# A hybrid decoder block: 64 bytes more in the tile hst, ahead of the weight slots

## The chip, the cores and the metric

The kernel runs on one core of one Trainium2 chip. Its time is the device time of one execution in microseconds (us), taken as the median of several runs. The profile is of one further execution. Five engines work side by side, each in its own order: TensorE (PE, whose weight loads are listed apart as PEld), VectorE (DVE), ScalarE (ACT), GpSimd (POOL) and SyncE (SP, which issues most DMAs). A matmul has a stationary operand, the weights, which a load of its own brings into the array, and a moving operand, whose rows stream past.

## What is computed

One layer of a decoder block for 2048 positions of 1024 channels. A projection `x @ W_in + b_in` with 72 x 128 output columns feeds two branches: dilated windowed attention with three head groups, and a gated linear recurrence (RG-LRU). Both are gated, merged, projected and normalised.

```
proj = x @ w_in[l] + b_in[l]
q, k, v, g_attn, u_lru, g_lru, gate_logits = jnp.split(proj, SPLIT_POINTS, axis=-1)
...
y_a = attn @ w_attn_proj[l]
...
u = causal_depthwise_conv(u_lru, conv_w[l], conv_b[l])
h = rg_lru(u, lru_wr[l], lru_br[l], lru_wi[l], lru_bi[l], lru_lambda[l]).astype(dt)
y_b = (h * jax.nn.silu(g_lru)) @ w_lru_proj[l]
...
merged = gates[:, :, 0] * y_a + gates[:, :, 1] * y_b
out = merged @ w_out[l] + b_out[l]
x = layer_norm(DEEPNORM_ALPHA * x + out, ln_gain[l], ln_bias[l])
```

In the recurrence, each position needs the state of the one before; the kernel works in chunks of 512 positions, and keeps each chunk's last column for the next.

## The kernel before, in words

**Three stages.** The first, up to about 1443 us, is the projection (the matmuls of line 647), with the recurrence woven in. The second, up to about 1837 us, is the attention and the product yb (line 1241). The last is ya (lines 1513 to 1515), the output product z (lines 1546 to 1548) and the normalisation.

**A pass of the projection.** The positions are taken in two halves, and in each half 36 passes s run over pairs of 128 output columns: 72 passes. Most passes use a scheme with seven products in place of eight: the two column blocks and the two halves of the 1024 channels make 2 x 2 blocks of weights, the channels and two chunks of 512 positions make 2 x 2 blocks of x, and sums of blocks are multiplied. The blocks of x, B11, B21, B12, B22 and the sums T1 to T4, appear in the profile as xB and xT, the weights as hA and hS, after the block or sum that they hold. Four passes, the first two of each half, run plainly with eight products. Their order is the list PLAIN, whose last two products both use B22:

```
PLAIN = [(fi, k, c) for c in range(2) for k in range(2) for fi in range(2)]
MID, EDGE = (1, 6, 7, 5, 2, 4, 3), (1, 2, 6, 7, 4, 5, 3)
```

In the other passes the last product, number 3, uses B22. The six others use blocks of x elsewhere.

**A product** (`product`) is 12 matmuls into one PSUM bank: for each of four groups of 128 channels the three terms high weights by high x, high weights by low x, low weights by high x. Such a triple reads as h, h, l in the profile. Every matmul brings its own weight load, which is 128 columns of 4 bytes (512 bytes a partition), while the moving operand has 512 columns (2048 bytes a partition). After six matmuls of a product the gates of the recurrence (lines 505 and 509: 6 matmuls each time, 32 times in all) may be put in.

**What sets the order.** The program is written out by hand for all engines: a loop of ticks, one product a tick, in which weights of later passes are loaded by SP, split into a high part by ACT (line 284) and a low part by DVE or POOL (line 240), results are taken out of PSUM, and chains of follow-up work are advanced.

**Where the operands stand.** Tiles of a pool follow each other in each partition, each beginning at a multiple of 32 bytes. Ahead of the pool sl_p stands the pool X, with six blocks of 16,384 bytes: seven of the eight blocks of x live there at one time or another, and all begin at the same place modulo 256. Then sl_p, in this order: slot 0 (2048 bytes), `ubs` (288), `hst` (64), the three tiles `ub0` to `ub2` of the recurrence (2064 each, so 2080), and the other 34 slots, the four tiles lo0 to lo3 for low weights (4096 each) and the block of B22, called XA (16,384), in the order of their first use. High weights take any free slot. The kernel takes 2048, 4096 or 16,384 bytes for each of these, so they all begin at one place modulo 256. Between the end of slot 0 and that place lie 288 + 64 + 3 x 2080 = 6592 = 25 x 256 + 192 bytes. So modulo 256:

- the six X blocks and slot 0 begin at one place;
- the other slots, the lo tiles and B22's block begin 64 bytes short of it;
- steps within them (512 bytes a weight tile, 2048 a moving row) are multiples of 256 and change nothing.

In the second and third stage sl_p is given up. The pools that follow begin where X ends, and the operands of yb, ya and z stand at the place of the X blocks, weights and moving rows alike.

`hst` holds for each of the eight channel tiles of the recurrence the last column of a chunk. It is cleared at the start (line 441), read as the initial state of the scan (line 546), and written by line 547. Only column 0 of its last dimension is used.

Of the kernel before, what the change touches and what calls it, by code (L numbers as in the profile page):

```python
# [8 lines left out]
F32 = mybir.dt.float32  # L9
# [6 lines left out]
P = 128  # L16
# [15 lines left out]
def hybrid_block_kernel(ctx: ExitStack, tc: tile.TileContext, a: dict, out: bass.AP):  # L32
# [111 lines left out]
    sl_p = stA.enter_context(tc.tile_pool(name="sl_p", bufs=1))  # L144
# [291 lines left out]

    lrn = cst.tile([P, 4, 8], F32, name="lrn")
    ubs = sl_p.tile([P, 8, 3, 3], F32, name="ubs")
    hst = sl_p.tile([P, 8, 2], F32, name="hst")
    dve.memset(ubs, 0.0)  # L440
    dve.memset(hst, 0.0)
    ub_free = [sl_p.tile([P, CH + 4], F32, name=f"ub{j}") for j in range(3)]
# [1228 lines left out]
```

## Time and profile before

| | |
|---|---|
| median of 3 runs | 2108.59 us (2106.66 to 2108.61) |
| the profiled execution's own time | 2111.93 us |
| its span | 2110.1 us |
| granted clock, mean | 0.997 |
| first stage, matmuls of line 647 | 7.2 to 1443.2 us, 6096 of them |
| DVE busy | 1695.4 us |
| DMA moved | 444.06 MB |

The span runs from the first to the last instruction of the profiled execution; that execution took 3.34 us more than the median. Times in the views are microseconds from the start of the span, unless marked ns. In the page, "xN" is a count, and an engine's busy share is of the whole span. A row of the timeline gives start, length, engine, line, operation, names (out<-in) and shape, and merges neighbours of one kind: "x2" are the two h terms of a triple. The ends of matmuls are modelled and overlap the next one's start; the starts are what is to be compared. A row of the windows gives the stretch, its length, busy time and number of instructions for each engine, then the granted clock, the share of the DMA engines' time and GB/s.

### The profile page before, as it was taken

Reading aid. Unit: us, or ns where it says so; the run is one execution under the profiler, and the core shown is the slowest. Engines: PE = TensorE matmul, PEld = TensorE weight load, DVE = VectorE, ACT = ScalarE, POOL = GpSimd, SP = SyncE. Lnnn points to the kernel's source line nnn. Section 1 sums busy time; section 2 is a strip of 40 time slices with the busy share of each in tenths; the row PEclk is TensorE's granted clock in tenths of the full one; section 3 lists DMA queues with packets and bytes.
Section 4 is the critical chain, followed back from the end, with each engine's and each line's share of the span. In section 5 each row is a group of like instructions: output and inputs, shape, how many; then the busy total and the mean of one; then the engine's idle time right before and its main releaser. Section 6 shows DMA issues by size and latency. Waiting matters only on the chain.

```text
span 2110.1 us, 35268 instructions
## 1 busy us (share of the span) xinstructions
PE 2088.1 (99%) x11877; PEld 1692.6 (80%) x11877; DVE 1695.4 (80%) x2985; ACT 1192.7 (57%) x2459; POOL 761.1 (36%) x685
## 2 busy tenths in 40 slices
PE   9999999999999999999999999999999999999998
PEld 7888888888888888888787888887878878788886
DVE  8878988999888858889788798975666776877667
ACT  6455455476457456767668877875666664321100
POOL 2554654545554201121120111114447678521120
PEclk9999999999999999999999999999999999999999
DMA  7877877788877766666657476669878886774431
GB/s 241 238 236 207 249 234 209 227 265 256 250 225 224 261 190 186 196 208 198 191 176 230 155 221 201 210 191 289 208 213 233 214 245 194 228 243 155 150 100 70
DMA packets 334180, 444.06 MB, mean 210 GB/s; under 512 B 164800, under 2 KB 174816, under 8 KB 330928
## 3 DMA queue, kind: packets, MB, share of 16 engines
q1 hardware_dynamic: 317360, 409.36, 62.2%
q0 software_dynamic: 11744, 23.54, 6.0%
q10 hardware_dynamic: 4896, 8.92, 1.1%
q8 instruction: 94, 1.54, 0.3%
q14 instruction: 86, 0.70, 0.1%
HBM read 290.20 MB, written 151.52 MB: 209 GB/s over the span
## 4 chain that ended last, share of the span: by engine, by line
PE 88%; DMA 3%; POOL 2%; SPq 2%; issue 2%; DVE 1%; ACT 1%; ACTq 0%; POOLq 0%; DVEq 0%
PE q L647 65%; PE yb L1241 4%; PE z L1547 3%; PE z L1546 3%; PE z L1548 3%; PE o L1071 2%; PE pt L1038 2%; PE s L1007 1%; PE g L505 1%; PE ya L1514 1%; PE ya L1515 1%; PE ya L1513 1%; POOL hx L1217 1%; DMA mg_scr<-y 1%; SPq L828 1%
## 5 line engine op out<-in xcount | busy, mean ns | idle before, releaser
L647 PE MATMUL q<-xT,hS 128*128 128x512 f32 x1632 | 507.0, 392 | 0.0
L647 PE MATMUL q<-xT,l 128*128 128x512 f32 x1088 | 426.9, 392 | 0.0
L647 PE MATMUL q<-xB,hA 128*128 128x512 f32 x1344 | 418.7, 393 | 0.0
L647 PE MATMUL q<-xB,l 128*128 128x512 f32 x944 | 370.5, 392 | 0.1
L647 PEld LDWEIGHTS q<-xT,hS 128*128 128x128 f32 x1632 | 305.7, 188 | 68.9 <-issue 4.0
L647 PEld LDWEIGHTS q<-xB,hA 128*128 128x128 f32 x1344 | 252.1, 188 | 57.1 <-issue 2.9
L647 PEld LDWEIGHTS q<-xT,l 128*128 128x128 f32 x1088 | 204.3, 188 | 46.9
L240 POOL TENSOR_TENSOR sw<-sw,sin 128x512 f32<-128x512 f32 x96 | 153.6, 1606 | 183.4 <-ACT sw L338 148.8
L647 PEld LDWEIGHTS q<-xB,l 128*128 128x128 f32 x944 | 177.2, 188 | 42.0 <-DVE l L240 0.5
L1023 ACT ACTIVATE pb<-pb 128x192 f32<-128x192 f32 (+1 forms) x384 | 160.7, 421 | 27.0 <-DVE pb L1021 27.0
L240 POOL TENSOR_TENSOR y<-y,h 128x512 f32<-128x512 f32 x27 | 35.6, 1318 | 383.9 <-DVE h L546 338.8
L647 PE MATMUL q<-xT,hA 128*128 128x512 f32 x544 | 169.5, 393 | 0.0
L647 PE MATMUL q<-xB,hS 128*128 128x512 f32 x544 | 169.3, 392 | 0.0
L284 ACT ACTIVATE hA<-wA 128x512 fp32r<-128x512 f32 x220 | 137.6, 636 | 38.2 <-PE q L647 17.4
L1241 PE MATMUL yb<-hx,wl 128*128 128x512 f32 x576 | 150.2, 401 | 1.9 <-POOL hx L1217 1.8
L240 POOL TENSOR_TENSOR l<-wA,hA 128x512 fp32r<-128x512 f32 x68 | 105.5, 1551 | 113.1 <-ACT hA L284 94.0
L284 ACT ACTIVATE hS<-S 128x512 fp32r<-128x512 f32 x170 | 108.2, 637 | 67.2 <-DVE S L240 52.3
L1241 PEld LDWEIGHTS yb<-hx,wl 128*128 128x128 f32 x576 | 104.9, 188 | 31.0 <-issue 6.1
L647 PEld LDWEIGHTS q<-xT,hA 128*128 128x128 f32 x544 | 101.7, 188 | 24.0 <-issue 2.6
L647 PEld LDWEIGHTS q<-xB,hS 128*128 128x128 f32 x544 | 102.1, 188 | 22.7
L1517 POOL TENSOR_TENSOR me<-gA,me 128x512 f32<-128x512 f32 x30 | 47.8, 1610 | 157.7 <-DVE gA L1516 135.4
L1546 PE MATMUL z<-wo,ms 128*128 128x512 f32 x256 | 99.6, 389 | 0.0
(215 smaller groups left out, 4307.5 us busy)
## 6 DMA issues: line engine op xcount, KB each, us to landing
wA<-in_w_in_dram SPq DMA_DIRECT2D x220, 256.0 KB
wl_scr<-l SPq DMA_DIRECT2D x102, 512.0 KB
l<-wl_scr SPq DMA_DIRECT2D x102, 512.0 KB
wS<-in_w_in_dram SPq DMA_DIRECT2D x102, 256.0 KB
wS<-in_w_in_dram POOLq DMA_DIRECT2D x68, 256.0 KB, 6.1
wlr<-in_w_f_dram SPq DMA_DIRECT2D x64, 256.0 KB
mg_scr<-y SPq DMA_DIRECT2D x59, 256.0 KB
v_scr<-vs SPq DMA_DIRECT2D x48, 256.0 KB
```

The lines of the kernel that those rows point to most:

```text
L240: eng.tensor_tensor(out=out, in0=in0, in1=in1, op=op)
L284: act.activation(heads(h), heads(r, False), AF.Copy)
L505: pe.matmul(g, gw[hs, l], x[hs], start=(n == 0), stop=(n == 2))
L647: pe.matmul(bank, w[:, ks], x[:, kk, xx], start=(first and i == 0), stop=(last and i == 11))
L1023: act.activation(pp, pp, AF.Exp, scale=-1.0, bias=mm, accum_out=ll)
L1038: pe.transpose(pt[e][:, b, 2 * h + x, :], pdata(p, h, c, c + P)[hs], ident[hs, hs])
L1071: pe.matmul(o[hs, 2 * i + b, :], (V[:, kb // 8, kb // 2 % 4, kb % 2] if g == 2 else V[:, kb % 2, kb // 4, kb // 2 % 2])[:, 64 * h:64 * h + ...
L1241: pe.matmul(YB["t"], w[:, a, k], hx(8 * c + k)[:, b], start=(hf == 0 and m == 0), stop=(hf == 1 and m == 11))
L1517: (dve if i in (6, 7) else pool).tensor_tensor(out=ME[c][:, f], in0=ga, in1=ME[c][:, f], op=ALU.add)
L1546: pe.matmul(z, mh[:, k], w[:, 0, hs], start=(k == 0), stop=False)
L1547: pe.matmul(z, mh[:, k], w[:, 1, hs], start=False, stop=False)
L1548: pe.matmul(z, ml[:, k], w[:, 0, hs], start=False, stop=(k == 7))
```

## The change

One number: the last dimension of `hst` is 4 in place of 2. Only column 0 is used as before. The tile takes 128 bytes a partition and not 64, and all that follows it in sl_p begins 64 bytes later; the X blocks, slot 0 and `ubs` stay. No instruction is added, removed or moved on any engine; the memset of line 441 covers 32 elements a partition and not 16.

```diff
     ubs = sl_p.tile([P, 8, 3, 3], F32, name="ubs")
-    hst = sl_p.tile([P, 8, 2], F32, name="hst")
+    hst = sl_p.tile([P, 8, 4], F32, name="hst")
     dve.memset(ubs, 0.0)
     dve.memset(hst, 0.0)
```

## The prediction

> **What bounds the kernel now.** First the page: its span, the busy share of each engine, the granted clock, and the chain of work that ended last.
>
> ```profile
> span 2110.1 us, 35268 instructions
> PE 2088.1 (99%) x11877; PEld 1692.6 (80%) x11877; DVE 1695.4 (80%) x2985; ACT 1192.7 (57%) x2459; POOL 761.1 (36%) x685
> ...
> PEclk9999999999999999999999999999999999999999
> ...
> PE 88%; DMA 3%; POOL 2%; SPq 2%; issue 2%; DVE 1%; ACT 1%; ACTq 0%; POOLq 0%; DVEq 0%
> ```
>
> The clock is granted in every slice, and 88% of the chain is TensorE itself. Next the busy time by stretches (us of the stretch, then busy us and instructions of PE and of PEld for line 647 alone) and the waits of PE up to 1450 us.
>
> ```profile
> 0.00:1450.00 1450.00, 1407.20 (x6096) 1143.13 (x6096) 1.00 0.72 219
> ```
>
> ```profile
> PE first_bank L858 <- ACT warm L850: 3.2, 1, 3.2
> PE pt L1038 <- ACT pb L1023: 1.3, 2, 1.2
> PE s L1001 <- DVE y L240: 0.4, 1, 0.4
> ```
>
> All 6096 matmuls of the projection lie in the first 1450 us, and no wait of PE for another engine is listed for line 647. So the projection lasts as long as 6096 matmuls follow each other, and the question is how closely they do. The page's busy time cannot tell, since the ends of matmuls are modelled. The starts can. Here is the timeline of PE over five products of one pass (start us, us, engine, line), first row and the row that begins the next product, both of the three-matmul pattern h, h, l:
>
> ```profile
> 467.83 0.62 PE L647 MATMUL q<-xT,hS 128*128 128x512 f32 x2
> ...
> 481.56 0.63 PE L647 MATMUL q<-xB,hS 128*128 128x512 f32 x2
> ```
>
> Between them stand 20 triples in 13.73 us: **0.6865 us a triple**, 228.8 ns a matmul. Weights and moving rows differ by 64 bytes (modulo 256) in these products. The same form of matmul (128 rows, 128 columns, 512 moving columns, three terms) runs in the last stage as z:
>
> ```profile
> 2057.56 0.39 PE L1546 MATMUL z<-wo,ms 128*128 128x512 f32 x1
> ...
> 2068.44 0.39 PE L1546 MATMUL z<-wo,ms 128*128 128x512 f32 x1
> ```
>
> 16 triples in 10.88 us: **0.6800 us a triple**, 226.7 ns a matmul, without an exception:
>
> ```profile
> L647 PE MATMUL q<-xT,hS x1632: 387/392/503, 54.2 to 1439.8; 128*128 128x512 f32 x182
> ...
> L1546 PE MATMUL z<-wo,ms x256: 389/389/389, 1861.2 to 2100.4; 128*128 128x512 f32 x128
> ```
>
> (least, median and longest ns of one.) For z, weights and rows begin at the same place within 256 bytes. That could be a trait of that stage, so the deciding rows are those of a product inside the projection that has the same property already: B22, whose block lies among the weight slots. In the plain pass at 737 us the last two products use it:
>
> ```profile
> 734.93 0.62 PE L647 MATMUL q<-xB,hA 128*128 128x512 f32 x2
> ...
> 737.67 0.63 PE L647 MATMUL q<-xB,hA 128*128 128x512 f32 x2
> ...
> 740.44 0.62 PE L647 MATMUL q<-xB,hA 128*128 128x512 f32 x2
> ...
> 743.16 0.63 PE L647 MATMUL q<-xB,hA 128*128 128x512 f32 x2
> ```
>
> Four triples with B12, 64 bytes apart, take 2.74 us; the first product with B22 takes 2.77, the second 2.72, which is 0.680 a triple as in z. Same engine, same line, same stage, same kind of weights; only the block changes, and the first product after the switch pays 0.05 to settle. So the spacing goes with the place modulo 256, and it needs some triples to find its state.
>
> **The change part by part.** It removes and moves no instruction. The memset of line 441 clears 32 elements a partition for 16, once, in the first microseconds, beside the loads that line 858 waits for anyway: nothing. Every tile of the pool behind hst moves up by 64 bytes, and 288 + 128 + 3 x 2080 = 6656 = 26 x 256 now lie between slot 0 and the rest: all weight slots, the four lo tiles and B22's block come to the place of the X blocks modulo 256. All 72 passes then run as the second B22 product did. Two edits come with it that I cost at nothing. The other engines mostly work from slot to slot, and these move together. DMAs into and out of slots begin 64 bytes further on; no row shows such a shift, but PE waits for none of them (the three waits above) at a DMA share of 0.72 in the windows' row, so a few per cent more or less on a transfer stay hidden; if that cover went, PE would wait for DMA by name.
>
> A whole pass of before, from the first row of one B22 product to that of the next, is 462.29 to 481.56:
>
> ```profile
> 462.29 0.63 PE L647 MATMUL q<-xB,hS 128*128 128x512 f32 x2
> ...
> 465.06 0.63 PE L647 MATMUL q<-xB,hA 128*128 128x512 f32 x2
> ...
> 465.77 0.62 PE L647 MATMUL q<-xB,hA 128*128 128x512 f32 x2
> ```
>
> It is 19.27 us for 28 triples; at 0.680 it is 19.04. The 0.23 us are 0.05 for the B22 product that has to settle (2.77 against 2.72), 0.03 for the triple behind it (0.71) and 23 triples at 0.0065. For 72 passes (four of them of 32 triples) that is 72 x 0.23 = **16.6 us**.
>
> Against it stand the interruptions. 32 pairs of gates are put into the middle of a product, and the spacing has to settle anew behind each. Now, 64 bytes apart, that is quick:
>
> ```profile
> 584.47 0.73 PE L647 MATMUL q<-xB,hA 128*128 128x512 f32 x2
> ...
> 585.27 0.62 PE L647 MATMUL q<-xB,hA 128*128 128x512 f32 x2
> ...
> 585.96 0.39 PE L647 MATMUL q<-xT,hS 128*128 128x512 f32 x1
> ```
>
> The triple behind the gates takes 0.80, the next 0.69. In the aligned state the nearest rows are yb's groups of twelve between other matmuls:
>
> ```profile
> 1473.49 3.01 PE L1241 MATMUL yb<-hx,wl 128*128 128x512 f32 x12
> 1476.43 0.46 PE L1038 MATMUL pt<-ident,pb 64*128 64x64 f32 x8
> ```
>
> 2.94 us for four triples, 0.22 over 2.72, of which the change of form at both ends has some 0.2 (the triple above has 0.11 at one end). So an interruption costs between 0.1 less and 0.1 more than now, 32 of them between -3 and +3 us; I take 0.03 each, as the B22 rows settle within 0.05: **-1.0 us**.
>
> The third term is what no longer hides. VectorE is the nearest engine behind:
>
> ```profile
> 400.00:500.00 100.00, 100.00 (x440) 81.21 (x440) 96.93 (x113) 60.23 (x100) 54.78 (x43) 1.00 0.86 253
> ```
>
> ```profile
> 372.70 0.69 DVE L537 SCALAR_TENSOR_TENSOR tr<-tr,e 128x512 f32<-128x512 f32 x1 [0.71 <-ACT sq L533]
> ...
> 398.98 1.78 DVE L240 TENSOR_TENSOR l<-wA,hA 128x512 fp32r<-128x512 f32 x1
> ...
> 401.12 0.39 PE L647 MATMUL q<-xT,l 128*128 128x512 f32 x1
> ```
>
> It is busy for 96.93 us of these 100 (third pair), and the low weights that it ends at 400.76 are read at 401.12, 0.36 us later. Its last gap was at 372.70, 28 us before, and in 28 us PE gains 1.2% (0.23 of 19.27), 0.34: the slack just holds. A wait of some tenths there and at one or two like places is what I charge: **-0.6 us**. From nothing to 4.8 us are possible (rival 2).
>
> Sum: 16.6 - 1.0 - 0.6 = 15.0 us, on the profiled execution 2111.93 - 15.0 = 2096.9. That execution lies 3.34 above the median of the runs, 2108.59, so the median to expect is **2093.6**. What follows the projection keeps its places and only begins earlier.
>
> **The rivals.** 1. No change. The spacing would go with the block or the stage and not with the place. For it: PEld shows 188 ns for a weight load everywhere, so the load itself is not slower 64 bytes apart. Against it: 2.74, 2.77 and 2.72 in three neighbouring products. It gives 2108.6. The Trainium skill has a rule that says so too (TensorE: Matmul & The Clock Gate, Step-by-step: what each phase is for): the array has two independent read ports on SBUF, and loading the next weights takes no read bandwidth from the running matmul. By it the place could not matter and the time would stay at 2108.6; the rows at 737 us speak against it.
>
> 2. VectorE becomes the bound, and takes part of the gain back. Its price is that PE gains nothing where VectorE is above 92%: the stretches 200 to 500 and 1200 to 1300 us, 400 us at 1.2% = 4.8 us.
>
> ```profile
> 200.00:300.00 100.00, 100.00 (x439) 81.41 (x438) 94.41 (x107) 53.03 (x86) 57.50 (x43) 1.00 0.83 244
> 300.00:400.00 100.00, 100.00 (x437) 81.69 (x436) 92.77 (x106) 53.27 (x85) 50.35 (x38) 1.00 0.71 216
> ...
> 1200.00:1300.00 100.00, 100.00 (x442) 80.44 (x441) 93.01 (x127) 72.77 (x116) 15.71 (x11) 1.00 0.69 213
> ```
>
> It gives 2093.6 + 4.8 = 2098.4. Against it: even 96.93 becomes only 98% of a stretch shorter by 1.2%.
>
> 3. Slower: the matmuls fall into a worse state and stay there. There is one in the trace:
>
> ```profile
> 504.73 0.63 PE L647 MATMUL q<-xB,hA 128*128 128x512 f32 x2
> ...
> 521.53 0.63 PE L647 MATMUL q<-xB,hS 128*128 128x512 f32 x2
> ```
>
> 24 triples in 16.80 us, 0.700 each. It began in a product whose weights stood in slot 0 and lasted until the next B22 product. If the aligned kernel ran in it throughout, a pass would take 19.60, 0.33 more than now, and 72 passes 23.8 us more: 2132.4. It decides the sign from the point where 0.23 x (1 - f) = 0.33 x f, f = 41% of the passes. Against it: it stands on pairs 64 bytes apart, B22 ended it, and z, always aligned, never leaves 389 ns.
>
> **How the numbers follow.** Forecast 80%: 2093.6, from 2090.5 (all 16.6 kept, with some luck in the settling) to 2097. Rival 2, or as much lost to ScalarE or transfers: 10%, 2097 to 2101. Rival 1: 6%. Rival 3: 4%. The range 2090.5 to 2099 holds the forecast's bounds and the better half of rival 2, some 85%, less what the run-to-run spread of 2 us (2106.66 to 2108.61) takes at its edges: 8 in 10. About 0.2%, 4.2 us, is what a measurement of this kernel can tell from no change. Faster by more is the forecast and rival 2, 90%; within it is rival 1, 6%; slower is rival 3, 4%.
>
> **What would show it.** Median of line 647's matmuls 389 ns, not 392, with PEld still at 188; a pass of 28 triples in 19.04 to 19.1 us; the first score matmul some 15 us earlier than now; the stages behind it as long as before; VectorE's busy time the same, on a shorter span. Wrong would be: 0.687 a triple as before (rival 1), a third spacing, new waits of PE on VectorE or ScalarE for line 647 of over 2 us in all (rival 2), or stretches at 0.700 (rival 3).

## The result, and the profile after

| | time, us | runs |
|---|---|---|
| before | 2107.62 median (2103.54 to 2108.61) | 4 |
| changed | 2091.55 median (2090.93 to 2092.82) | 4 |
| ratio | 0.9928, 95% interval 0.9911 to 0.9945 | |

The changed kernel is 16.07 us faster; the interval reaches from 11.6 to 18.8 us. The profiled execution of the changed kernel took 2092.82 us. Its page, span, busy shares, clock and chain:

```profile
span 2091.0 us, 35268 instructions
PE 2070.6 (99%) x11877; PEld 1692.0 (81%) x11877; DVE 1703.0 (81%) x2985; ACT 1191.7 (57%) x2459; POOL 764.4 (37%) x685
...
PEclk9999999999999999999999999999999999999999
...
PE 73%; DMA 3%; DVE 2%; POOL 1%; issue 1%; SPq 1%; ACT 1%; POOLq 0%; DVEq 0%; ACTq 0%
```

The count of instructions is the same, the clock is granted in every slice as before, and PEld is busy just as long (1692.0 for 1692.6). The shares of the chain can't be set side by side: they add up to 99% before and to 82% after, since the chain after could be followed back only to a row of VectorE at 388.56 us. So the 15 points that PE has less there are no finding. The page's busy time of PE is still 99% and says nothing. The view of line 647's instructions (least, median and longest ns):

```profile
L647 PEld LDWEIGHTS q<-xT,hS x1632: 186/188/190, 53.8 to 1425.8; 128*128 128x128 f32 x182
L647 PE MATMUL q<-xT,hS x1632: 389/389/501, 54.1 to 1426.1; 128*128 128x512 f32 x182
```

The matmul's median is now z's 389 ns, the weight load keeps its 188. The starts of a whole pass, in the timeline of PE:

```profile
458.62 0.61 PE L647 MATMUL q<-xB,hS 128*128 128x512 f32 x2
...
461.33 0.61 PE L647 MATMUL q<-xB,hA 128*128 128x512 f32 x2
...
464.06 0.61 PE L647 MATMUL q<-xT,hS 128*128 128x512 f32 x2
...
474.94 0.61 PE L647 MATMUL q<-xT,hA 128*128 128x512 f32 x2
...
477.65 0.61 PE L647 MATMUL q<-xB,hS 128*128 128x512 f32 x2
```

From B22 to B22 the pass takes 19.03 us (19.27 before). The product with B22 takes 2.71 and the next one 2.73, so nothing is left to settle behind the switch of the block. The 16 triples from 464.06 to 474.94 take 10.88 us, 0.680 each, z's spacing to the digit.

The projection ends where the first score matmul (line 1001) begins. Before, then after:

```profile
1443.20 0.49 PE L1001 MATMUL s<-qk 64*128 64x128 f32 x2
```

```profile
1429.33 0.48 PE L1001 MATMUL s<-qk 64*128 64x128 f32 x2
```

So the two profiled executions differ by **13.87 us** in the projection. The second stage, from there to the first ya (start of the first and of the last one in this view), before and after:

```profile
L1513 PE MATMUL ya<-at,wa x128: 388/389/397, 1839.4 to 2046.0; 128*128 128x512 f32 x128
```

```profile
L1513 PE MATMUL ya<-at,wa x128: 388/389/397, 1820.2 to 2026.9; 128*128 128x512 f32 x128
```

It lasted 396.2 us before and 390.9 after. The runs below don't show that the change speeds this stage up; these 5.3 us are one execution against one. The ya loop takes 206.6 and 206.7.

Two waits for VectorE are listed that were not listed before. The waits of PE up to 1429 us (us in total, times, longest), then rows of the timeline of PE and VectorE at both:

```profile
PE first_bank L858 <- ACT warm L850: 3.2, 1, 3.2
PE q L647 <- DVE l L240: 1.3, 2, 0.8
```

```profile
369.60 0.69 DVE L537 SCALAR_TENSOR_TENSOR tr<-tr,e 128x512 f32<-128x512 f32 x1 [0.71 <-ACT sq L533]
...
395.84 1.77 DVE L240 TENSOR_TENSOR l<-wA,hA 128x512 fp32r<-128x512 f32 x1
...
397.66 0.50 PE L647 MATMUL q<-xT,l 128*128 128x512 f32 x1 [0.75 <-DVE l L240]
...
720.43 0.50 PE L647 MATMUL q<-xB,l 128*128 128x512 f32 x1 [0.57 <-DVE l L240]
```

The first row of PE is the very place that the prediction watched at 401.12. The low weights are ready at 397.61, and PE, which now wants them at 396.91 (397.66 less the wait), stands still for 0.75 us.

### The profile page after: what moved, and what is told of

It is laid out like the page before. It is cut to its first block, busy times and chain, and to the rows that moved or that the text cites. A ratio compares the mean times of both kernels' runs of the same rounds, so it can differ in the third digit from the quotient of the medians.

```text
span 2091.0 us, 35268 instructions
## 1 busy us (share of the span) xinstructions
PE 2070.6 (99%) x11877; PEld 1692.0 (81%) x11877; DVE 1703.0 (81%) x2985; ACT 1191.7 (57%) x2459; POOL 764.4 (37%) x685
## 4 chain that ended last, share of the span: by engine, by line
PE 73%; DMA 3%; DVE 2%; POOL 1%; issue 1%; SPq 1%; ACT 1%; POOLq 0%; DVEq 0%; ACTq 0%
PE q L647 47%; PE yb L1241 7%; PE o L1071 3%; PE z L1547 3%; PE z L1546 3%; PE z L1548 3%; PE pt L1038 2%; PE s L1007 2%; PE ya L1514 1%; PE ya L1515 1%; PE g L505 1%; PE ya L1513 1%; DMA mg_scr<-y 1%; PE s L1001 1%; SPq L828 1%
```

## The experiments

Two theories stood against each other at first. **Relative place**: the spacing depends on where weights and moving rows begin within 256 bytes, relative to each other. **Absolute place** or period: it depends on where the slots begin as such, or on another period than 256. Later a third question came up: whether each weight load pays for itself. In all kernels below, "apart" gives the place of weights, lo tiles and B22 relative to the X blocks, modulo 256 if nothing else is said; slot 0 and the X blocks stay together. Each first-score row shows where the projection ended.

**Everything moved, still 64 short.** A 64-byte tile ahead of X moves X and slots together, so the slots stand where they stand in the changed kernel, but still 64 bytes short of the X blocks.

```diff
     lrn = cst.tile([P, 4, 8], F32, name="lrn")
+    gap = cst.tile([P, 16], F32, name="gap")
+    dve.memset(gap, 0.0)
```

> hst as before (64 bytes), and 64 bytes more in a pool ahead of the X blocks, so that X blocks, slot 0 and all slots move up by 64 together: the slots begin where the changed kernel has them in memory, and still stand 64 bytes short of the X blocks modulo 256. If the place of weights and rows relative to each other decides, nothing is gained: 0.687 us a triple, line 647's matmuls at a median of 392 ns, the first score matmul near 1443 us, the time as before, 2107.6 within 3. If the place of the slots alone decides (their start, or what DMAs and other engines make of it), it is as the changed kernel: 0.680, 389 ns, 1429 us, 2091.6.

2106.25 us median of 10 runs against 2107.57 of 14 of the kernel before: ratio 0.9994 (0.9985 to 1.0003). Its first score matmul (the line number is two higher):

```profile
1443.52 0.49 PE L1003 MATMUL s<-qk 64*128 64x128 f32 x2
```

A shift of the absolute place by 64 bytes does nothing that these runs can tell. The same goes for the shift by 64 bytes of every transfer into and out of slots, which the prediction had costed at nothing without a row.

**32 bytes to either side.** One element less and one more in `hst` than in the changed kernel: 32 short and 32 past.

```diff
-    hst = sl_p.tile([P, 8, 4], F32, name="hst")
+    hst = sl_p.tile([P, 8, 3], F32, name="hst")
```

> hst of 96 bytes: slots, lo tiles and B22's block stand 32 bytes short of the X blocks modulo 256 (64 before, 0 in the changed kernel). If the cost grows with the distance, the spacing lies between: some 0.683 us a triple, the projection's end near 1436 us. If anything but 0 costs the same, 0.687 as before, near 1443 us. If lines of 64 bytes are what has to agree, worse than both is possible, since before was a multiple of 64 and this is not.

> hst of 160 bytes: the slots stand 32 bytes past the X blocks' place modulo 256. If only the distance counts, as the kernel that is 32 short (between 0.680 and 0.687 a triple). If the order counts (weights ahead of the rows or behind them), the two differ. The rival that any rise of the slots' address helps expects 0.680, as it is 32 bytes above the changed kernel.

2134.54 and 2133.98 us, one run each. The view of line 647 and the first score matmul for 32 short, then the latter for 32 past:

```profile
L647 PE MATMUL q<-xT,hS x1632: 389/396/497, 54.6 to 1459.4; 128*128 128x512 f32 x182
```

```profile
1462.73 0.48 PE L1001 MATMUL s<-qk 64*128 64x128 f32 x2
```

```profile
1461.92 0.49 PE L1001 MATMUL s<-qk 64*128 64x128 f32 x2
```

Both lie some 19 us behind the kernel before, though they are nearer to agreement than its 64 bytes. The distance does not set the cost; agreement does. Half the distance is worse than the whole.

**256 bytes apart within 512.** `ubs` goes to the pool ahead of X, and `hst` takes 160 bytes: the place modulo 256 is that of the X blocks, modulo 512 it is 256 bytes off.

```diff
-    ubs = sl_p.tile([P, 8, 3, 3], F32, name="ubs")
-    hst = sl_p.tile([P, 8, 4], F32, name="hst")
+    ubs = cst.tile([P, 8, 3, 3], F32, name="ubs")
+    hst = sl_p.tile([P, 8, 5], F32, name="hst")
```

> ubs goes to the pool ahead of the X blocks and hst has 160 bytes: the slots then stand 25 x 256 bytes from slot 0's end and not 26 x 256, so they agree with the X blocks modulo 256 but not modulo 512 (256 apart there). If 256 is the period, all is as in the changed kernel: 0.680 us a triple, median 389 ns, first score matmul near 1429 us, 2091.6 us within 2. If 512 is the period, this is the kernel furthest from agreement: 0.687 or more for the X blocks, 2107 us or more.

2097.86 us median of 5 runs (2093.19 to 2100.41), ratio 0.9953 (0.9938 to 0.9968).

```profile
L647 PE MATMUL q<-xT,hS x1632: 389/389/500, 53.6 to 1425.5; 128*128 128x512 f32 x182
```

```profile
1428.73 0.49 PE L1001 MATMUL s<-qk 64*128 64x128 f32 x2
```

In the projection it is the changed kernel: 389 ns and the same end within 0.6 us. So places that differ by 256 are alike, and the period is not 512. Half of 256 is not alike, since 128 bytes apart cost time (below): the period is 256. Its whole time is 6 us above the changed kernel's median, though; more on that below.

**64 past and 128.** For 64 past, `hst` takes 192 bytes and the two one-column tiles `half_t` and `one_t` share one, to make room; for 128, `hst` goes to the pool ahead of X. Both edits also move the X blocks and slot 0, by 32 and by 64 bytes; the two kernels above that move them, by 64 and by 288 bytes, show no cost of that.

```diff
-    hst = sl_p.tile([P, 8, 4], F32, name="hst")
+    hst = sl_p.tile([P, 8, 6], F32, name="hst")
```

```diff
-    hst = sl_p.tile([P, 8, 4], F32, name="hst")
+    hst = cst.tile([P, 8, 2], F32, name="hst")
```

> hst of 192 bytes, and the two constants half_t and one_t in one tile to make room: the slots stand 64 bytes past the X blocks' place modulo 256, the mirror image of before (64 short). If the distance alone counts: 0.687 us a triple, the projection's end near 1443 us. If the order counts, another spacing, with 0.700 (the state that the trace of before shows in one pass) as the likeliest other value: then near 1470 us.

> hst goes to the pool ahead of the X blocks: the slots stand 128 bytes from the X blocks' place modulo 256, half a period. If the cost grows with the distance, it is the worst place: above 0.687 us a triple, the projection's end beyond 1443 us. If anything but 0 costs the same: 0.687, near 1443. If 128 is the period: 0.680, near 1429.

2125.89 and 2125.26 us, one run each, beside 2109.70 for the kernel before on that chip. For 64 past, rows of the timeline and the first score matmul; for 128, the latter:

```profile
473.82 0.63 PE L647 MATMUL q<-xT,hS 128*128 128x512 f32 x2
...
485.02 0.63 PE L647 MATMUL q<-xT,hA 128*128 128x512 f32 x2
...
487.82 0.62 PE L647 MATMUL q<-xB,hS 128*128 128x512 f32 x2
...
490.56 0.63 PE L647 MATMUL q<-xB,hA 128*128 128x512 f32 x2
...
1461.83 0.48 PE L1001 MATMUL s<-qk 64*128 64x128 f32 x2
```

```profile
1460.14 0.48 PE L1001 MATMUL s<-qk 64*128 64x128 f32 x2
```

16 triples in 11.20 us: 0.700 each, pass after pass. That is the state of rival 3 (24 triples in 16.80 us). It exists, and here it belongs to a place apart. It does not hold throughout: the product at 485.02 takes 2.80 us, but the next one, at 487.82, takes 2.74. It is the one with B22, whose block stands with the slots, so that its rows agree with its weights even here. Over the whole projection the median triple of this kernel is 0.680 in the products with B22 that close a pass and 0.700 in all the others of the pass. So the place of weights and rows decides within one kernel, too, with everything else the same. 64 past is not the mirror image of 64 short: 0.700 against 0.6865.

**Which loads pay.** Two thirds of the matmuls take high weights, one third low ones. From the kernel before, the lo tiles alone are allocated right behind slot 0, so that only the high weights (and B22's block) stay 64 short:

```diff
+    for i in range(NL):
+        dve.memset(sl_p.tile([P, 2, CH], F32, tag=f"lo{i}", name=f"first{i}")[:, 0, 0:1], 0.0)
     ubs = sl_p.tile([P, 8, 3, 3], F32, name="ubs")
```

> hst as before; the four lo tiles are given their place right behind slot 0, so that the low weights agree with the X blocks modulo 256 and only the high weights (and B22's block) stand 64 bytes short. In a triple h, h, l two of the three weight loads are of high weights. If each load pays for its own distance to the rows that stream meanwhile, two thirds of the cost remain: 0.6847 us a triple, the projection's end near 1438 us. If a single agreeing pair is enough to settle the whole triple, 0.680 and near 1429 us; if a single one apart spoils it, 0.687 or worse, 1443 us or later.

In the second kernel the lo tiles stand behind the `ub` tiles, 64 short, and a 64-byte tile behind them brings the other slots into agreement, so that only the low weights are apart:

```diff
     ub_free = [sl_p.tile([P, CH + 4], F32, name=f"ub{j}") for j in range(3)]
+    for i in range(NL):
+        dve.memset(sl_p.tile([P, 2, CH], F32, tag=f"lo{i}", name=f"first{i}")[:, 0, 0:1], 0.0)
+    gap = sl_p.tile([P, 16], F32, name="gap")
+    dve.memset(gap, 0.0)
```

> The reverse: the lo tiles are given their place ahead of 64 bytes more, so that only the low weights stand 64 bytes short, and high weights, B22's block and X blocks agree modulo 256. One load in three is apart. If each load pays for itself: 0.6822 us a triple, the projection's end near 1434 us. If one agreeing pair is enough: 0.680, near 1429. If one apart spoils the triple: 0.687 or worse, 1443 us or later.

2110.01 and 2119.72 us, one run each, beside the same 2109.70. The first score matmul with the high weights alone apart, then two rows of the timeline and the first score matmul with the low ones alone apart:

```profile
1444.92 0.49 PE L1003 MATMUL s<-qk 64*128 64x128 f32 x2
```

```profile
471.30 0.62 PE L651 MATMUL q<-xT,hS 128*128 128x512 f32 x2
...
482.40 0.62 PE L651 MATMUL q<-xT,hA 128*128 128x512 f32 x2
...
1453.54 0.48 PE L1005 MATMUL s<-qk 64*128 64x128 f32 x2
```

Bringing a third of the matmuls into agreement saves nothing: 1444.92 against 1443.20. Bringing two thirds into it makes it worse: 16 triples in 11.10 us, 0.694 each, and the projection ends 10 us later than with all apart. So the theory that each misplaced load pays its own share falls. One kind of weights apart is enough to lose the spacing of all three matmuls: from start to start their medians are 0.229 to 0.233 us in these two kernels, for 0.227 in agreement. The cost belongs to the sequence and not to the single load.

**The waits for VectorE taken away.** From the changed kernel, three low weight tiles (those of the two waits and one more) are made by POOL and not by VectorE.

```diff
+            late_low = (s, j) in ((19, 5), (21, 5), (36, 2))
+            eng = pool if late_low else eng
...
-                if eng is pool:
+                if eng is pool and not late_low:
```

> The changed kernel, with three of the low-weight subtractions (the second plain half's third weight tile at 720 us, and the sixth tile of passes 19 and 21, at 398 and 436 us) on GpSimd and not on VectorE, as GpSimd is idle there by the trace. If VectorE's queue is what TensorE waits for at 397 and 720 us, the two waits (0.75 and 0.57 us with what they do to the spacing behind them: 1.03 and 0.85) go: the first score matmul some 1.5 us earlier, near 1427.6 us, and the time some 1.5 us lower, near 2090, which the clock of the runs can hardly tell from the changed kernel's 2091.6. If something else holds these weights back (the load, or ScalarE's copy), the waits stay, under another name.

2092.33 us median of 4 runs, ratio 0.9926 (0.991 to 0.9943). The waits of PE up to 1428 us, the POOL row that replaces the late one of VectorE, and the first score matmul:

```profile
PE first_bank L860 <- ACT warm L852: 3.2, 1, 3.2
PE g L507 <- DVE vl L240: 0.3, 1, 0.3
```

```profile
395.25 1.71 POOL L240 TENSOR_TENSOR l<-wA,hA 128x512 fp32r<-128x512 f32 x1 [0.72 <-ACT hA L284]
```

```profile
1427.28 0.48 PE L1003 MATMUL s<-qk 64*128 64x128 f32 x2
```

Both waits of line 647 are gone, and the projection ends 2.05 us earlier than in the changed kernel's first profile, 0.92 earlier than in the one below, and 15.92 earlier than in the first profile of the kernel before. The list names another wait in their place, of the gates (line 507) for the low part `vl` that VectorE makes. The median does not show the gain; 1 to 2 us is below what these runs tell apart.

**The kernels once more.** The kernel before, the changed one and the one with 256 bytes apart, unchanged, to see how much two executions of one kernel differ.

> The kernel before, profiled once more, for the length of the stages. The median of the time fell by 16.1 us, the projection in the two profiles by 13.9 (1443.2 to 1429.3), so some 2 us are to be found behind it. If the second stage (from the first score matmul to the first ya matmul: 396.2 us before, 390.9 in the changed kernel, 389.5 in the kernel with both moved) merely varies from execution to execution, it is here anywhere from 389 to 397, and the projection ends at 1443.2 to 1443.6 again. If the place of hst shortens it, it is 394 or more here.

> The changed kernel once more, beside the kernel before on the same chip. The projection ends at 1429.3 within 0.5 us, with the two waits for VectorE near 397 and 720 us at the same places. If the second stage only varies, it is anywhere from 389 to 397 us; if the change shortens it, at most 392.

> The kernel with the slots 256 bytes from agreement modulo 512, once more: its projection ended at 1428.7 as the changed kernel's, but its median was 2097.9, 6 us above. If its second stage varies more, this execution may show 389 to 400 us there with the projection at 1428.7 again. If its projection has a second, slower state that the first profile missed, it ends at 1432 or later here.

2109.00, 2091.77 and 2095.61 us. Their first score matmuls, in that order, with the only wait of line 647 that is listed for the changed kernel in this execution behind its row (in the waits, and in the timeline):

```profile
1442.38 0.48 PE L1001 MATMUL s<-qk 64*128 64x128 f32 x2
```

```profile
1428.20 0.48 PE L1001 MATMUL s<-qk 64*128 64x128 f32 x2
```

```profile
PE q L647 <- DVE l L240: 0.3, 1, 0.3
```

```profile
719.33 0.50 PE L647 MATMUL q<-xB,l 128*128 128x512 f32 x1 [0.34 <-DVE l L240]
```

```profile
1429.02 0.48 PE L1001 MATMUL s<-qk 64*128 64x128 f32 x2
```

All kernels side by side. The projection's end is the start of the first score matmul; the second stage runs from there to the first ya.

| weights relative to X blocks | projection ends, us | second stage, us |
|---|---|---|
| all 64 short (before, again, all moved) | 1443.2, 1442.4, 1443.5 | 396.2, 394.2, 389.5 |
| agree (changed, again; 256 of 512, again) | 1429.3, 1428.2; 1428.7, 1429.0 | 390.9, 391.1; 392.2, 393.9 |
| agree, three low tiles on POOL | 1427.3 | 393.4 |
| high weights and B22 64 short | 1444.9 | 392.9 |
| low weights alone 64 short | 1453.5 | 393.6 |
| 128 apart | 1460.1 | 393.2 |
| 64 past | 1461.8 | 392.1 |
| 32 past, 32 short | 1461.9, 1462.7 | 399.6, 399.2 |

The first column sorts by place, with 1.1 us between executions of one place. The mean of the first row is 1443.0, that of the second 1428.8: **14.2 us** of the 16.07 are the projection's, and these are shown. The second column doesn't sort by whether the places agree: 389.5 to 396.2 where they stand as before, 390.9 to 393.9 where they agree. The interval of the whole gain (11.6 to 18.8 us) holds the 14.2 by themselves. Whether the remaining 1.9 us are more than the spread of the second stage is not settled. The same goes for the 6 us by which the kernel with 256 of 512 lies above the changed one while its projection ends together with it, and for the 399 us of the kernels with 32 bytes.

## Why the prediction held, step by step

Predicted: 15.0 us less, 2093.6. Measured: 16.07 less, 2091.55. The mechanism was the right one; the terms were not all of the right size.

**A pass of 28 triples at 0.680, 16.6 us over 72 passes.** The pass of the prediction came out at 19.03 for 19.04. The order of the matmuls is the same in both kernels, so all 2032 triples of the projection can be set side by side, from start to start. All but five of them together gain 16.03 us in the first pair of executions (before, changed) and 15.96 in the second. Between the two executions of the kernel before, the same triples differ by 0.01 us, so this is the spacing and not the spread. The term was about 0.6 too large. What it overcharged is the switch of the block: the products with B22 and the triple behind each gained 4.5 us, where 72 x 0.08 = 5.8 were taken. The other triples gained 11.6 for 72 x 23 x 0.0065 = 10.8.

**Interruptions by the gates, -1.0 us.** In the aligned state, on the same pair of gates that was measured before:

```profile
579.04 0.73 PE L647 MATMUL q<-xB,hA 128*128 128x512 f32 x2
...
579.84 0.62 PE L647 MATMUL q<-xB,hA 128*128 128x512 f32 x2
...
580.53 0.62 PE L647 MATMUL q<-xT,hS 128*128 128x512 f32 x2
```

The triple behind the gates takes 0.80 and the next 0.69, as before. It is so at all 32 places: the triples that hold the gates and the two behind each, all but one of them, together gain 0.55 us (counted in the 11.6 above). So the term is 0, where 1.0 was charged.

**Waits for VectorE, -0.6 us.** This term was too small. The five triples left out above lose 2.17 us in the first pair and 1.61 in the second. Three of them wait for VectorE. The two of the list lose 1.02 and 0.50 in the first pair, 0.27 and 0.61 in the second. (At the second place the kernel before had stood still a little as well: its triple at 726.33 takes 1.03 us.) The third is not listed under line 647, because there the gates wait, for `vl`; it loses 0.24 and 0.36. VectorE's row that makes `vl` and the weight load of the gates that needs it, before and after:

```profile
439.57 1.19 DVE L240 TENSOR_TENSOR vl<-v,vh 128x512 fp32r<-128x512 f32 x1
...
440.82 0.19 PEld L505 LDWEIGHTS g<-vl,gw 64*128 64x128 f32 x2
```

```profile
436.13 1.19 DVE L240 TENSOR_TENSOR vl<-v,vh 128x512 fp32r<-128x512 f32 x1
...
437.38 0.19 PEld L505 LDWEIGHTS g<-vl,gw 64*128 64x128 f32 x2 [0.29 <-DVE vl L240]
```

Before, `vl` was ready at 440.76 and the load began at 440.82, with no idle time ahead of it. Now `vl` is ready at 437.32, 3.44 us earlier; PE is 3.78 earlier here (the triple at 436.11 for 439.89), and its load stands idle for 0.29. So VectorE costs 1.8 us in the first pair and 1.2 in the second, not 0.6. The other two triples are the first one of the projection, which takes 0.70 to 1.28 us in the three executions with the places of before, too, and one at 1190.05 that waits for high weights of ScalarE and loses 0.1.

The step that failed is the sentence that PE gains 0.34 us in 28 and the slack just holds. It counted what PE gains since VectorE's last gap, as if the gap itself moved with PE. It doesn't: the row of line 537 moved from 372.70 to 369.60, 3.10 us earlier, while PE wants the low weights at 396.91 for 401.12, 4.21 earlier. 4.21 - 3.10 = 1.11 us, less the slack of 0.36, is the 0.75 of the wait. VectorE was not in step with PE. What it was in step with shows just ahead of the gap, in the timeline of POOL and VectorE, before and after:

```profile
360.57 1.30 POOL L240 TENSOR_TENSOR y<-y,h 128x512 f32<-128x512 f32 x1 [3.15 <-DVE h L546]
...
364.24 1.93 POOL L240 TENSOR_TENSOR sw<-sw,sin 128x512 f32<-128x512 f32 x1
...
365.37 1.36 DVE L529 SCALAR_TENSOR_TENSOR ti<-ti,v 128x512 f32<-128x512 f32 x1 [2.14 <-ACT ti L525]
```

```profile
357.82 1.31 POOL L240 TENSOR_TENSOR y<-y,h 128x512 f32<-128x512 f32 x1 [3.15 <-DVE h L546]
...
361.48 1.93 POOL L240 TENSOR_TENSOR sw<-sw,sin 128x512 f32<-128x512 f32 x1
...
361.61 2.36 DVE L529 SCALAR_TENSOR_TENSOR ti<-ti,v 128x512 f32<-128x512 f32 x1 [1.14 <-ACT ti L525]
```

VectorE's instruction of line 529 begins 3.76 us earlier than before, and ends only 2.76 earlier: in both traces 0.56 us after POOL's, which itself moved by 2.76. It takes 1.36 and 2.36 us here, while the median of this line is 0.69. The Trainium skill (SBUF — State Buffer, SBUF: two separate sides) says that VectorE with two operands from SBUF and a GpSimd instruction that reads SBUF share a pair of ports as an exclusive lock, and that the later one waits for the whole instruction of the first; these rows agree. Behind it, VectorE's next low weights took 1.14 us for 1.49, and ScalarE, which ends the gap, had waited for these: so the gap moved by 3.10. An engine that seems to have slack of its own stands where its neighbours let it. POOL in its turn had waited for the scan of VectorE (line 546), which came 2.75 us earlier; what held the scan was not traced. That the waits came from VectorE's low weights, and are gone when POOL makes them, is shown by the experiment for the two places of line 647.

**The sum.** In the first pair the projection gained 16.03 - 2.17 us, which is the 13.87 of the profiles but for the rounding. Predicted were 15.0. That this lies so near the measured 16.07 is in part luck: the 1.0 charged too much for the gates stands against some 0.6 too much for the spacing and 1.6 too little for the five triples, and some 1.9 us of the measured gain have no place in the sum.

**What the memset and the shifted transfers cost: nothing.** Shown by the kernel in which all moved.

**What follows keeps its places and only begins earlier.** It holds for the third stage. For the second, two executions of one kernel differ by up to 2.0 us, and the whole spread for the places of before is 6.7; the prediction's "as long as before" can't be tested finer than that.

**The rivals.** *No change*: fallen, 13.87 us in the projection. The row that spoke for it, 188 ns for every weight load, holds in all kernels (medians of 187 to 188) and says nothing: the load's own length does not grow while the spacing does. By the rule of the Trainium skill (TensorE: Matmul & The Clock Gate, Step-by-step: what each phase is for), two independent read ports for rows and weights, the place could not matter; the end of the projection at 1428.8 or 1462.7, by place alone, is against it as far as the spacing goes. *VectorE becomes the bound*: the mechanism occurs, for 1.2 to 1.8 us and not 4.8. VectorE is busy for 1703.0 us now and was for 1695.4, where the prediction had it unchanged. *The 0.700 state*: real, at 64 past in every pass but for the products with B22. Where places agree, the median triple of every product is 0.680. It would have decided the sign had the change been 32, 96 or 128 bytes and not 64.

## What to carry to other kernels

All this is shown for weight loads of 128 columns of 4 bytes under 512 moving columns, and for no other form. Where every matmul brings its own weight load, compute from the allocation where stationary and moving operands begin modulo 256 bytes, and make them agree; a filler of some bytes in a small tile does it. Make all of them agree: a part of them in agreement gained nothing here or lost. A shift that goes only part of the way may cost more than it gains, so read the spacing from starts of neighbouring matmuls, since the page's busy share and the weight load's length do not show it.

## What was not expected of the hardware

- The cost of being apart is not a function of the distance: per triple 0.680 in agreement, 0.6865 at 64 short, 0.700 at 64 past, and at 32 short the projection ends latest of all. The pair -64 and +64 gives 14 and 33 us over the projection of the aligned kernel.
- One misplaced matmul in three (the low weights) costs more, 0.694 a triple, than all three misplaced the same way, 0.6865.
- The spacing changes while the weight load stays at 187 to 188 ns. What inside TensorE or its reads makes the spacing depend on the place is not settled by these runs.
- The spacing repeats far better than the time: two executions of the kernel before differ by 0.6 us from the first triple of the projection to its last, all of it in two triples, and by 0.01 us in the rest.
